# Attention with buffers of its own for the weights before normalising, and a different order around the first scores and the products with values

## The chip, the cores and the metric

The kernel runs on one core of a Trainium2 chip. The metric is the device time of one execution in microseconds (us). The core's engines work side by side, each through its own instructions in order: TensorE (PE) multiplies matrices, VectorE (DVE) and ScalarE (ACT) work element by element, SyncE (SP) issues the transfers, GpSimd (POOL) does little here.

## The reference, cut to what matters

A trunk of two layers over 512 tokens of width 1024, in float32. Layer 0 mixes tokens by native sparse attention, layer 1 by a gated linear recurrence; each mixer stands between two half-step feed-forward networks, and a layer norm follows each of these six parts. The change is in the attention of layer 0:

```python
h = x @ w_in
q, k_c, v_c, k_s, v_s, k_w, v_w, gate = jnp.split(h, ...)
...
o_c = jnp.einsum('bgqtn,bgnd->bgqtd', p_c.astype(dt), vc)
...
l_s = jnp.einsum('bgqtd,bgtsd->bgqts', qb, k_g).astype(F32) * scale + b_s
p_s = _masked_softmax(l_s, (d_s >= 0)[:, :, None])
o_s = jnp.einsum('bgqts,bgtsd->bgqtd', p_s.astype(dt), v_g)
...
return (gb[..., 0:1] * o_c + gb[..., 1:2] * o_s + gb[..., 2:3] * o_w).astype(dt)
...
return o @ w_out
```

There are 16 heads in 4 groups; a group shares its keys and values. Each query has three attentions (over compressed blocks, over selected blocks, over a window), summed with gates. With 512 tokens all blocks are selected and the window reaches over everything, so that the second and third are two causal softmaxes with different keys and values (t = 0 and 1 in the code).

## The kernel before, in words

**Stage.** `nsa_body` first projects keys, values and gates for all groups. Then comes the part that the change touches. Its work is cut into 64 units, in the order: group (4), pair of heads in the group (2), tile of 128 queries `i` (4), head of the pair (2). A pair has 8 units; pair k ends as units 8k to 8k+7 are done.

**Steps.** The loop over n runs in steps; in step n it does, in this order, parts of several units:

- `att_e` for unit n−2: two exponentials on ACT (line 904) turn the scores into unnormalised weights `pe` and sum them up for the denominator (`den`);
- the copies of the product of an earlier step from PSUM to `o` and `o1` on ACT (line 939), queued in `self.last`;
- `att_b` for unit n−3: PE transposes `pe` in blocks of 128x128 (line 917), four to a PSUM bank; ACT copies the first bank to `pt` (line 920), DVE the second (line 922);
- what the tables place at this step (`side`, below);
- `att_a` for unit n: PE computes scores from queries `qs` and keys `kh`, `kl` (lines 882 and 883, 128 queries by up to 512 keys for each t) into banks `sc`; DVE takes the minimum of the far scores (889), adds the bias `near` and takes the minimum (891), whose result `nm` is the exponentials' offset (scores are negated);
- `att_c` for units n−5 and n−4, in odd n−4: PE multiplies the transposed weights with the values into `po` (line 935).

PE executes in the order in which the program is written. The order on the other engines is set by the framework's scheduler, and a transfer waits until its buffer is free.

**PSUM** has 4 banks for scores (`psc`), 3 for all else (`ps`) and 1 for `po`.

**Weights.** `weight` (lines 125 to 135) loads 512 KB into a buffer of `self.raw`, which has three; ACT writes the rounded half `whi` (line 124) and DVE the rest `wlo` (line 125), both into `self.wr`. A product is three matmuls (141 to 143). `self.raw` also holds `rev`, the bias table of a group before it is turned round into `near` (lines 538 to 543), and `pe`.

**Tables.** `PRE` lists what is projected before the first unit: two key weights and the first half (two heads) of group 0's queries. `PLAN` places, for each group, the loads and projections in steps: for groups 1 to 3 the list `Q` relative to step 0, 16 and 32 (load at 0, query projections at 3 and 8, scores against compressed keys at 10 and 11), for group 2 also the keys of groups 2 and 3 (`K`). `FIN` places the end of pair k, relative to step 8k: `factors` (reciprocals of `den` times the gates, DVE), `turned` (PE transposes them, ACT and DVE write them as `rt`, lines 770 to 772), `weigh(0)` and `weigh(1)` (PE spreads `rt` over the head's rows, line 776; DVE multiplies `o` or `o1` by it, 778, and adds both, 780), `compressed` (the first attention's product, 784 and 785) and `o_split`. What lies past the last step is done inside the output projection that follows (`out_proj`).

## Time and profile before

| what | value |
|---|---|
| time, median of 3 runs | 2057.42 us (2056.58 to 2058.37) |
| the profiled execution's own time | 2057.78 us |
| its span, first to last instruction | 2056.0 us |
| mean granted TensorE clock | 0.995 of full speed |
| PE busy | 2005.1 us (98%) |
| DVE busy | 1384.1 us (67%) |
| ACT busy | 1007.4 us (49%) |
| moved by transfers | 193.92 MB, mean 94 GB/s |

The profile is of one execution. The 1.8 us between its time and its span lie before the first and after the last instruction. PE's busy time counts pipelined matmuls as busy from their start to a modelled end. The part that the change touches runs from about 415 to 655 us of the span. In a timeline row the number in square brackets is the time for which the engine stood idle before the instruction, and the arrow names what released it; in the views of waits such times are summed.

### The profile page before, as it was taken

How to read it: one execution, taken by the hardware profiler on the slowest of the kernel's cores; microseconds unless marked ns; L12 is line 12 of the kernel's file. 1: busy time of each engine (PE TensorE's matmuls, PEld its weight loads, DVE VectorE, ACT ScalarE, POOL GpSimd, SP SyncE). 2: the span in 40 equal slices, each digit the busy share in tenths (PEclk: the TensorE clock that was granted, in tenths of full speed). 3: DMA queues.
4: the chain of work that ended last, by engine and by line, in shares of the span. 5: the costliest groups of instructions: out<-in, count | busy, mean ns of one | idle time of the engine just before them, and what ended most of it. 6: DMA issues, size and time to landing. Idle time of an engine off the chain costs nothing.

```text
span 2056.0 us, 36186 instructions
## 1 busy us (share of the span) xinstructions
PE 2005.1 (98%) x15225; PEld 1803.7 (88%) x15225; DVE 1384.1 (67%) x1996; ACT 1007.4 (49%) x1670; POOL 142.0 (7%) x165
## 2 busy tenths in 40 slices
PE   9999999999999999999999999999999999999998
PEld 9998998877777899899899989988887779998996
DVE  8845866366777797477599558663735868955864
ACT  5542553246677355245345435534736844543551
POOL 0000002000000200000020000030412112000002
PEclk9999999999999999999999999999999999999999
DMA  5342342311103235133334423422220043342331
GB/s 185 124 144 62 104 134 70 106 40 42 42 1 114 93 109 174 47 103 93 113 97 130 144 62 103 139 88 90 87 84 2 4 144 103 121 147 62 103 124 41
DMA packets 138768, 193.92 MB, mean 94 GB/s; under 512 B 8572, under 2 KB 117564, under 8 KB 138605
## 3 DMA queue, kind: packets, MB, share of 16 engines
q1 hardware_dynamic: 138604, 191.61, 30.1%
q8 instruction: 119, 1.95, 0.4%
q14 instruction: 45, 0.36, 0.1%
HBM read 189.40 MB, written 2.19 MB: 93 GB/s over the span
## 4 chain that ended last, share of the span: by engine, by line
PE 80%; DVE 11%; ACT 3%; issue 3%; DMA 2%; POOL 1%; SPq 0%; POOLq 0%; DVEq 0%; ACTq 0%
PE ps L141 24%; PE ps L142 23%; PE ps L143 23%; DVE wlo L125 2%; PE ps L364 2%; PE ps L917 2%; PE po L935 1%; DMA fr<-in_ffn_w_up_dram 1%; DVE raw L395 1%; PE sc L882 1%; DVE xl L125 1%; PE ps L183 1%; PE sc L883 1%; POOL ry L220 1%; DVE x L230 1%
## 5 line engine op out<-in xcount | busy, mean ns | idle before, releaser
L125 DVE TENSOR_TENSOR wlo<-raw,whi 128x1024 fp32r<-128x1024 f32 (+1 forms) x253 | 310.9, 1233 | 247.0 <-ACT whi L124 246.6
L124 ACT ACTIVATE whi<-raw 128x1024 fp32r<-128x1024 f32 (+1 forms) x253 | 266.0, 1056 | 324.3 <-PE ps L143 144.8
L141 PE MATMUL ps<-xh,whi 128*128 128x256 f32 (+1 forms) x992 | 296.1, 299 | 1.3 <-ACT xh L124 0.5
L142 PE MATMUL ps<-xl,whi 128*128 128x256 f32 (+1 forms) x992 | 294.6, 297 | 0.7 <-DVE xl L125 0.7
L143 PE MATMUL ps<-xh,wlo 128*128 128x256 f32 (+1 forms) x992 | 294.1, 296 | 0.0
L143 PE MATMUL ps<-whi,xlo 128*128 128x512 f32 x704 | 274.4, 390 | 1.5 <-DVE xlo L125 1.5
L141 PE MATMUL ps<-whi,xhi 128*128 128x512 f32 x704 | 274.4, 390 | 0.0
L142 PE MATMUL ps<-wlo,xhi 128*128 128x512 f32 x704 | 274.0, 389 | 0.0
L141 PEld LDWEIGHTS ps<-xh,whi 128*128 128x128 f32 x992 | 187.7, 189 | 9.7 <-ACT xh L124 1.0
L142 PEld LDWEIGHTS ps<-xl,whi 128*128 128x128 f32 x992 | 187.6, 189 | 7.9 <-DVE xl L125 1.1
L143 PEld LDWEIGHTS ps<-xh,wlo 128*128 128x128 f32 x992 | 187.5, 189 | 6.7
L124 ACT ACTIVATE whi<-fr 128x1024 fp32r<-128x1024 f32 x120 | 126.1, 1061 | 115.4 <-PE ps L142 80.7
L141 PE MATMUL ps<-xh,xhi 128*128 128x256 f32 x640 | 177.6, 278 | 2.7 <-DVE c L450 2.7
L142 PE MATMUL ps<-xl,xhi 128*128 128x256 f32 x640 | 177.2, 277 | 0.0
L143 PE MATMUL ps<-xh,xlo 128*128 128x256 f32 x640 | 177.2, 277 | 0.0
L125 DVE TENSOR_TENSOR wlo<-fr,whi 128x1024 fp32r<-128x1024 f32 x120 | 145.6, 1221 | 44.9 <-ACT whi L124 44.7
L143 PEld LDWEIGHTS ps<-whi,xlo 128*128 128x128 f32 x704 | 132.1, 188 | 30.6 <-DVE xlo L125 3.2
L395 DVE TENSOR_TENSOR raw<-fr 128x1024 f32<-128x1024 f32 x120 | 145.7, 1222 | 17.8 <-DMA fr<-in_ffn_w_up_dram 16.3
L141 PEld LDWEIGHTS ps<-whi,xhi 128*128 128x128 f32 x704 | 132.2, 188 | 26.9
L142 PEld LDWEIGHTS ps<-wlo,xhi 128*128 128x128 f32 x704 | 132.2, 188 | 26.9
L125 DVE TENSOR_TENSOR xlo<-h,xhi 128x1024 fp32r<-128x1024 f32 x44 | 53.9, 1226 | 110.8 <-ACT xhi L124 110.8
L141 PEld LDWEIGHTS ps<-xh,xhi 128*128 128x128 f32 x640 | 120.4, 188 | 3.5 <-DVE c L450 3.5
(279 smaller groups left out, 4635.3 us busy)
## 6 DMA issues: line engine op xcount, KB each, us to landing
raw<-in_ffn_w_down_dram SPq DMA_DIRECT2D x88, 512.0 KB, 3.6
fr<-in_ffn_w_gate_dram SPq DMA_DIRECT2D x80, 512.0 KB, 4.0
fr<-in_ffn_w_up_dram SPq DMA_DIRECT2D x80, 512.0 KB, 5.1
raw<-in_hgrn_w_in_dram SPq DMA_DIRECT2D x32, 512.0 KB, 4.1
raw<-in_nsa_w_in_dram SPq DMA_DIRECT2D x18, 512.0 KB, 3.8
raw<-in_ffn_w_gate_dram SPq DMA_DIRECT2D x8, 512.0 KB, 4.6
raw<-in_ffn_w_up_dram SPq DMA_DIRECT2D x8, 512.0 KB, 4.9
raw<-in_nsa_w_out_dram SPq DMA_DIRECT2D x8, 512.0 KB, 4.5
```

The source lines that it names most:

```text
L124: a = self.nc.scalar.activation(hi, src, AF.Copy)
L125: b = self.nc.vector.tensor_tensor(lo, src, hi.bitcast(F32), op=ALU.subtract)
L141: mm(out, l[0], r[0], start=start, stop=False)
L142: mm(out, l[0], r[1], start=False, stop=False)
L143: mm(out, l[1], r[0], start=False, stop=stop)
L183: self.nc.tensor.transpose(p[:, j, :], self.x[c][:, k * P : (k + 1) * P], self.ident)
L220: self.nc.gpsimd.tensor_tensor(y, y, self.mhalf[:, :n], op=ALU.pow)
L230: nc.vector.scalar_tensor_tensor(x[:, s], x[:, s], float(scale), banks[h], op0=ALU.mult, op1=ALU.add)
L364: nc.tensor.matmul(out, l, xx, start=k == low == 0 and xx is x[0], stop=k == 7 and low == 1)
L395: tt(out, x, y, op=op)
L882: nc.tensor.matmul(sc, l, kh[g][:, ts[0] : ts[0] + x, :n], start=True, stop=False)
L917: nc.tensor.transpose(p[:, j * P : j * P + P], pf[:, (b0 + j) * P : (b0 + j + 1) * P], self.ident)
```

## The change

1. `pe` moves from `self.raw` to two buffers of its own in the attention's pool. The space comes from `pt` (4 buffers to 3), `near` (2 buffers of 4 heads to 3 of 2 heads) and `o1` (2 to 1).
2. `near` is written as two tiles of two heads each by two DVE copies; for groups 1 to 3 its load moves from step 0 of the group's list to step 9.
3. The second half of group 0's queries is projected before the first unit instead of at step 2.
4. In a step, the products with values (`att_c`) come ahead of the scores (`att_a`).
5. At the end of a pair `weigh(1)` comes first, at step 12, then `weigh(0)` at 13, which now also adds `o1`; `compressed` moves from 14 to 15.

```diff
--- before.py
+++ after.py
@@ -52,12 +52,12 @@
 LB = 3
 LC = 4
 
-PRE = [("keys", 0), ("keys", 1), ("queries", 0)]
-Q = [(0, "load", "q"), (3, "queries", 0), (8, "queries", 1), (10, "cmp_a", 0), (11, "cmp_a", 1), (24, "cmp_b")]
+PRE = [("keys", 0), ("keys", 1), ("queries", 0), ("queries", 1)]
+Q = [(0, "load", "q"), (3, "queries", 0), (8, "queries", 1), (9, "load", "near"), (10, "cmp_a", 0), (11, "cmp_a", 1), (24, "cmp_b")]
 K = [(5, "load", 0), (7, "load", 1), (10, "keys", 0), (11, "keys", 1)]
-PLAN = [(0, 0, [(2, "queries", 1), (4, "cmp_a", 0), (4, "cmp_a", 1), (10, "cmp_b")]), (1, 0, Q), (2, 16, Q + K), (3, 32, Q)]
-
-FIN = [(10, "factors", ()), (11, "turned", ()), (13, "weigh", (0,)), (14, "compressed", ()), (15, "weigh", (1,)), (17, "o_split", ())]
+PLAN = [(0, 0, [(4, "cmp_a", 0), (4, "cmp_a", 1), (10, "cmp_b")]), (1, 0, Q), (2, 16, Q + K), (3, 32, Q)]
+
+FIN = [(10, "factors", ()), (11, "turned", ()), (12, "weigh", (1,)), (13, "weigh", (0,)), (15, "compressed", ()), (17, "o_split", ())]
 
 
 class Trunk:
@@ -538,8 +538,9 @@
         rev = self.raw.tile([P, 4, 256], F32, name="rev", tag="raw")
         nd = self.near_d
         nc.sync.dma_start(rev, bass.AP(tensor=nd.tensor, offset=nd.offset + 4 * g * 384, ap=[[1, P], [384, 4], [1, 256]]))
-        near = pool.tile([P, 4, 256], F32, name="near", tag="near", bufs=2)
-        nc.vector.tensor_copy(near, rev[:, :, ::-1])
+        near = [pool.tile([P, 2, 256], F32, name="near", tag="near", bufs=3) for _ in range(2)]
+        for i, t in enumerate(near):
+            nc.vector.tensor_copy(t, rev[:, 2 * i : 2 * i + 2, ::-1])
         return near
 
     def nsa_cb(self, pool):
@@ -687,7 +688,7 @@
             nc.gpsimd.memset(pc, 0.0)
             cb = self.nsa_cb(pool)
             prep = [self.group_prep(pool, w, g, groups[g], pc, cb) for g in range(4)]
-            for t in ("q", 0, 1):
+            for t in ("near", "q", 0, 1):
                 prep[0]["load"](t)
             work = self.ps
             for f, *x in PRE:
@@ -725,7 +726,7 @@
                 exps = []
                 if LE <= n < len(units) + LE:
                     g, hh, i = units[n - LE]
-                    pes[n - LE], exps = self.att_e(opool, groups[g], hh, i)
+                    pes[n - LE], exps = self.att_e(pool, groups[g], hh, i)
                 behind, self.last = self.last, []
                 with self.after(exps[-1:]):
                     for f in behind:
@@ -734,12 +735,12 @@
                         pts[n - LB] = self.att_b(pool, units[n - LB][2], pes.pop(n - LB))
                 for f in side.pop(n, ()):
                     f()
+                if n >= LC and (n - LC) % 2:
+                    g, hh, i = units[n - LC]
+                    self.att_c(opool, groups[g], g, hh // 2, i, [pts.pop(n - LC - 1), pts.pop(n - LC)])
                 if n < len(units):
                     g, hh, i = units[n]
                     self.att_a(pool, g, groups[g], hh, i)
-                if n >= LC and (n - LC) % 2:
-                    g, hh, i = units[n - LC]
-                    self.att_c(opool, groups[g], g, hh // 2, i, [pts.pop(n - LC - 1), pts.pop(n - LC)])
             for f in self.last:
                 f()
             assert not side
@@ -776,8 +777,8 @@
             nc.tensor.matmul(p, spread[:, t].rearrange("p x d -> p (x d)"), rt, start=True, stop=True)
             own = (out, st["o1"][pr])[t]
             tt(own, own, p, op=ALU.mult)
-            if t:
-                tt(out, out, own, op=ALU.add)
+            if t == 0:
+                tt(out, out, st["o1"][pr], op=ALU.add)
 
         def compressed():
             p = self.psum()
@@ -796,8 +797,9 @@
         v, vc, gate, kc, o = self.kv
 
         def load(t):
-            if t == "q":
+            if t == "near":
                 st["near"] = self.nsa_near(pool, g)
+            elif t == "q":
                 st["us"] = self.units(w, 256 * g, 256)
                 st["q"], st["den"], st["o1"], st["sc"] = [], [], [], {}
             else:
@@ -873,7 +875,7 @@
         n = (i + 1) * P
         l = st["q"][hh][:, i * P : i * P + P]
         m = min(n, 256)
-        bias = st["near"][:, hh, 256 - m :]
+        bias = st["near"][hh // 2][:, hh % 2, 256 - m :]
         nm = self.small.tile([P, 2], F32, name="nm", bufs=6)
         out = []
         for ts in ((0, 1),) if i < 2 else ((0,), (1,)):
@@ -898,7 +900,7 @@
             st["den"].append(self.small.tile([P, NT, 2, 2], F32, name="den", bufs=3))
         den = st["den"][hh // 2]
         out, nm = st["sc"].pop((hh, i))
-        pe = self.raw.tile([P, 2, (i + 1) * P], F32, name="pe", tag="raw")
+        pe = pool.tile([P, 2, (i + 1) * P], F32, name="pe", tag="pe", bufs=2)
         exps = []
         for t in range(2):
             ins = self.nc.scalar.activation(pe[:, t, :], out[t], AF.Exp, scale=-1.0, bias=nm[:, t : t + 1], accum_out=den[:, i, hh % 2, t : t + 1])
@@ -908,7 +910,7 @@
     def att_b(self, pool, i, pe):
         nc = self.nc
         nb = 2 * (i + 1)
-        pt = pool.tile([P, nb, P], F32, name="pt", tag="pt", bufs=4)
+        pt = pool.tile([P, nb, P], F32, name="pt", tag="pt", bufs=3)
         pf = pe.rearrange("p t n -> p (t n)")
         for b0 in range(0, nb, 4):
             m = min(4, nb - b0)
@@ -927,7 +929,7 @@
         nc = self.nc
         v, vc, gate, kc, o = self.kv
         if i == 0:
-            st["o1"].append(pool.tile([P, T], F32, name="o1", tag="o1", bufs=2))
+            st["o1"].append(pool.tile([P, T], F32, name="o1", tag="o1"))
         po = self.po[:, i % 2]
         for t in range(2):
             for j in range(i + 1):
```

What the steps become on the engines' instruction lists:

**ACT, the end of group 0's units and the start of group 1's.** `whi<-raw` is the split of a weight, `pe` the exponentials (128x512 of the last units of group 0, 128x128 of the first of group 1), `pt` copies of transposed weights, `o` copies of the product. Before:

```order
L920 ACTIVATE pt<-ps 128x512
L124 ACTIVATE whi<-raw 128x1024
L904 ACTIVATE pe,den<-sc,nm 128x512
L124 ACTIVATE whi<-raw 128x1024
L904 ACTIVATE pe,den<-sc,nm 128x512
L920 ACTIVATE pt<-ps 128x512
L904 ACTIVATE pe,den<-sc,nm 128x128 x2
L939 ACTIVATE o<-po 128x128
L939 ACTIVATE o_4859<-po 128x128
```

Now:

```order
L941 ACTIVATE o<-po 128x128
L941 ACTIVATE o_4854<-po 128x128
L922 ACTIVATE pt<-ps 128x512
L906 ACTIVATE pe,den<-sc,nm 128x512 x2
L922 ACTIVATE pt<-ps 128x512
L906 ACTIVATE pe,den<-sc,nm 128x128 x2
L941 ACTIVATE o<-po 128x128
L941 ACTIVATE o_4854<-po 128x128
L922 ACTIVATE pt<-ps 128x512
```

The two splits of group 2's query weights have left this place; the exponentials stand together.

**SP, the loads of the stage.** `raw` are weights, `rev` the bias table of a group, `cb` that of the compressed keys. Before:

```order
L540 DMA rev<-near_d 128x4x256
L550 DMA cb<-cmp_d 16x16x56 x8
L133 DMA raw<-in_nsa_w_in_dram 128x4x256 x2
L540 DMA rev<-near_d 128x4x256
L133 DMA raw<-in_nsa_w_in_dram 128x4x256 x2
L133 DMA raw<-in_nsa_w_in_dram 128x8x128 x2
L540 DMA rev<-near_d 128x4x256
L133 DMA raw<-in_nsa_w_in_dram 128x4x256 x2
L133 DMA raw<-in_nsa_w_out_dram 128x1024 x6
```

Now:

```order
L133 DMA raw<-in_nsa_w_in_dram 128x4x256
L551 DMA cb<-cmp_d 16x16x56 x8
L133 DMA raw<-in_nsa_w_in_dram 128x4x256
L540 DMA rev<-near_d 128x4x256
L133 DMA raw<-in_nsa_w_in_dram 128x4x256 x2
L133 DMA raw<-in_nsa_w_in_dram 128x8x128 x2
L540 DMA rev<-near_d 128x4x256
L133 DMA raw<-in_nsa_w_in_dram 128x4x256 x2
L540 DMA rev<-near_d 128x4x256
L133 DMA raw<-in_nsa_w_out_dram 128x1024 x7
```

The bias tables of groups 1 to 3 now follow the query weights of the groups, and one more weight of the output projection stands ahead of what follows the stage.

**PE, steps 12 to 14, the end of the first pair.** `po<-pt,v` are products with values, `sc` scores, `ps<-ident,pe` transposes, `ps<-rt,spread` the product of `weigh`, `ps<-pct,vc` that of `compressed`. Before:

```order
L917 MATMUL ps<-ident,pe 128x128 x4
L776 MATMUL ps<-rt,spread 128x512
L882 MATMUL sc<-kh,qs 128x384
L883 MATMUL sc<-kl,qs 128x384
L882 MATMUL sc<-kh,qs 128x384
L883 MATMUL sc<-kl,qs 128x384
L935 MATMUL po<-pt,v_3612 64x128 x4
L917 MATMUL ps<-ident,pe 128x128 x4
L784 MATMUL ps<-pct,vc 128x512
```

Now:

```order
L919 MATMUL ps<-ident,pe 128x128 x2
L777 MATMUL ps<-rt,spread 128x512
L884 MATMUL sc<-kh,qs 128x384
L885 MATMUL sc<-kl,qs 128x384
L884 MATMUL sc<-kh,qs 128x384
L885 MATMUL sc<-kl,qs 128x384
L919 MATMUL ps<-ident,pe 128x128 x4
L777 MATMUL ps<-rt,spread 128x512
L937 MATMUL po<-pt,v_3612 64x128 x4
L884 MATMUL sc<-kh,qs 128x384
```

The first `spread` product now stands behind the two transposes of step 12, the second behind the four of step 13, and the products with values ahead of the scores.

## Rows read from the trace of the kernel before

**Rows 1.** The page, busy time by engine, and its group of weight splits on DVE.

```profile
PE 2005.1 (98%) x15225; PEld 1803.7 (88%) x15225; DVE 1384.1 (67%) x1996; ACT 1007.4 (49%) x1670; POOL 142.0 (7%) x165
...
L125 DVE TENSOR_TENSOR wlo<-raw,whi 128x1024 fp32r<-128x1024 f32 (+1 forms) x253 | 310.9, 1233 | 247.0 <-ACT whi L124 246.6
```

**Rows 2.** Stretches: length, busy us of PE, PEld, DVE, ACT, POOL; clock, DMA share, GB/s.

```profile
454.00:462.00 8.00, 5.64 (x43) 3.65 (x39) 8.00 (x37) 6.02 (x19) 0.00 (x0) 1.00 0.00 0
...
490.00:502.00 12.00, 7.79 (x38) 6.13 (x35) 5.73 (x17) 7.45 (x23) 0.00 (x0) 0.72 0.22 76
...
556.00:568.00 12.00, 7.79 (x50) 6.29 (x49) 6.57 (x20) 7.45 (x23) 0.00 (x0) 0.86 0.29 88
...
sum 240.00, PE 223.84 PEld 177.01 DVE 177.80 ACT 155.38 POOL 0.00; mean PE 22.38 PEld 17.70 DVE 17.78 ACT 15.54 POOL 0.00
```

**Rows 3.** What PE waited for, 415 to 660: us in total, times, longest.

```profile
PE ps L917 <- ACT pe L904: 8.4, 4, 2.8
...
PE sc L882 <- ACT pe L904: 3.3, 5, 1.1
...
PE sc L882 <- DVE qs L826: 2.7, 2, 1.5
...
PE ps L141 <- ACT o L939: 0.6, 1, 0.6
```

**Rows 4.** Timeline of PE: start, length, line, tiles; idle time before and releaser.

```profile
493.53 0.66 PE L917 MATMUL ps<-ident,pe 128*128 128x128 f32 x4 [2.77 <-ACT pe L904]
...
495.62 1.12 PE L917 MATMUL ps<-ident,pe 128*128 128x128 f32 x4 [1.44 <-ACT pe L904]
...
560.42 0.66 PE L917 MATMUL ps<-ident,pe 128*128 128x128 f32 x4 [2.80 <-ACT pe L904]
```

**Rows 5.** Timeline of all engines at the first stall (SPq: SP's DMA queue).

```profile
488.01 1.50 SPq L133 DMA_DIRECT2D raw<-in_nsa_w_in_dram  x2
...
491.75 1.06 ACT L124 ACTIVATE whi<-raw 128x1024 fp32r<-128x1024 f32 x1 [3.41 <-DMA raw<-in_nsa_w_in_dram]
```

**Rows 6.** What SP's queue waited for, 360 to 700.

```profile
SPq L133 <- PE ps L917: 116.1, 9, 88.5
```

**Rows 7.** Stretches of 2 us, columns as in rows 2.

```profile
436.00:438.00 2.00, 2.00 (x7) 1.61 (x6) 0.97 (x5) 2.00 (x6) 0.00 (x0) 0.59 0.01 4
...
494.00:496.00 2.00, 0.56 (x4) 0.38 (x3) 1.40 (x4) 2.00 (x5) 0.00 (x0) 0.59 0.00 0
...
496.00:498.00 2.00, 2.00 (x9) 1.70 (x8) 1.47 (x6) 2.00 (x11) 0.00 (x0) 0.50 0.00 0
...
500.00:502.00 2.00, 2.00 (x8) 1.60 (x7) 0.00 (x0) 0.00 (x0) 0.00 (x0) 0.70 0.00 0
...
562.00:564.00 2.00, 1.51 (x6) 1.37 (x7) 1.65 (x3) 2.00 (x10) 0.00 (x0) 0.66 0.00 0
```

**Rows 8.** Timeline of PE, first and last matmul of an undisturbed query projection.

```profile
583.98 0.50 PE L141 MATMUL ps<-xh,whi 128*128 128x512 f32 x1
...
589.32 0.40 PE L143 MATMUL ps<-xh,wlo 128*128 128x512 f32 x1
```

**Rows 9.** Timeline of PE, scores waiting for a bank in odd steps.

```profile
459.29 0.50 PE L882 MATMUL sc<-kh,qs 128*128 128x512 f32 x1 [0.59 <-ACT pe L904]
...
480.32 0.44 PE L882 MATMUL sc<-kh,qs 128*128 128x384 f32 x1 [0.44 <-ACT pe L904]
```

**Rows 10.** Timeline of PE, DVE and ACT around the end of the first pair.

```profile
477.49 0.68 DVE L772 TENSOR_TENSOR rt<-ps,rt 4x512 fp32r<-4x512 f32 x1
...
477.52 0.42 PE L882 MATMUL sc<-kh,qs 128*128 128x384 f32 x1
...
482.61 0.43 ACT L939 ACTIVATE o<-po 128x128 f32<-128x128 f32 x2
...
487.01 0.68 DVE L780 TENSOR_TENSOR o<-o,o 128x512 f32<-128x512 f32 x1
```

**Rows 11.** Timeline of ACT at the end of the stage.

```profile
649.45 2.05 ACT L124 ACTIVATE whi<-raw 128x1024 fp32r<-128x1024 f32 x2
```

## Prediction

> **What bounds the kernel now.** I began with the page: over the whole span TensorE (PE) is busy for 98%, VectorE (DVE) for 67% [rows 1]. A change that removes no matmul can only gain where PE stands still or runs slowly, so I next cut the attention stage (about 415 to 655 us of the span) into stretches. Two of twelve microseconds stand out, 490 to 502 and 556 to 568: in each PE works 7.79 us, at a mean granted clock of 0.72 and 0.86; and between 454 and 462 it is DVE that is full, 8.00 of 8.00; over the whole stage PE is idle for 240 − 223.84 = 16.2 us [rows 2]. Then I asked what PE waits for. The largest entry is the transposes of the unnormalised weights (`ps`, line 917) waiting for ACT's exponentials (`pe`): 8.4 us in four waits. After it come scores waiting for exponentials (3.3 us in five: their PSUM banks are still being read), scores waiting for `qs` (2.7 in two) and the output projection waiting for the last copy of `o` (0.6) [rows 3].
>
> The timeline of PE places the 8.4 us: 2.77 and 1.44 near 493 us, 2.80 and the remaining 1.4 near 560 us [rows 4]. ACT shows why. Between two exponentials stands the split of a weight, `whi<-raw`, and ACT sat idle for 3.41 us until that weight's load landed; the loads were issued only at 488.01 [rows 5]. They could not go earlier: `pe` and weight loads rotate through the same three buffers of `raw`, so a load waits until the transposes have read an old `pe`. SP waited 116.1 us for those transposes in all [rows 6]. ACT executes in its order, so the exponentials behind `whi` wait for a load that has nothing to do with them.
>
> The stall costs twice. PE waits, and then it runs at the lower granted clock: 0.59 in the window that starts at 494, 0.50 from 496 to 500, 0.70 in the window after [rows 7]; 0.50 is the 1.2 GHz level, 1.00 the 2.4 GHz level. The same fall follows the pause before the first scores: 0.59 from 436 to 438 and about the same in the two us after [rows 7].
>
> **The change, part by part.** The profiled execution took 2057.78 us, 0.36 above the median of the runs. I sum against 2057.78.
>
> *Own buffers for `pe`.* With `pe` out of `raw`, SP can issue the loads of groups 2 and 3 much earlier, and the order on ACT shows the effect: no `whi` is left among the exponentials of units 15 and 31, the last of groups 0 and 1. Both stalls should go. First: idle 2.77 + 1.44 = 4.21; at the low clock, lost share times PE's busy time, 0.41 × 0.56 + 0.5 × 2 + 0.5 × 2 + 0.3 × 2 = 2.83 [rows 7], the window from 498 like the one from 496. Second: idle 2.80 + 1.4 = 4.2; clock 0.34 × 1.51 [rows 7] + 0.5 × 2 for the window after it = 1.5. Together 7.04 + 5.7 = **−12.7**. A lower bound for what is lost is the idle time alone, 8.4. No matmul, exponential or load is added or dropped here.
>
> *Where the loads go instead.* The splits of group 2's queries and first key weight now stand in the first steps, and those of the output weights in the attention stage. Each costs 1.06 us on ACT and 1.23 on DVE [rows 1, 5]. Most stand next to a projection of 24 matmuls, which keeps PE busy by itself for 5.74 us (583.98 to 589.72) [rows 8]. The tight one is the key weight at step 5: its load takes the buffer that the split of a query weight frees. That split ends some 2.2 us into the projection (1.0 for work ahead of it, an estimate, and 1.23); the load takes 3.74 from issue to the start of `whi` (488.01 to 491.75), and 1.06 + 1.23 follow: 8.2 us, against 5.74 of projection and about 1.5 of scores and transposes behind it. I take **+1.0**, bounds 0 and 2.5 (8.2 − 5.74).
>
> *Second query projection ahead of the first scores.* Before, PE pauses 1.46 + 1.22 us for `qs` (the 2.7 of [rows 3]) and then loses 0.41 × 2 by the clock in one window and about as much in the next, 1.6: 4.3 in all. Afterwards the first scores find the first `qs` long ready, but the pause may return at the first transposes: ACT must finish the copies of the second projection and a `whi` before it comes to the first exponentials. All 24 matmuls run in either version. I take **0**, the pause coming back in the size that it has now: the 2.7 is the nearest row. Bounds: −3.3 (one us of pause is left) and +2.2 (a `whi` and a DVE copy more).
>
> *Products with values ahead of the next scores.* Of the five waits of scores for a bank, those of odd steps, 0.59 and 0.44 among them [rows 9], now have products in front of them. They sum to 1.5 at most. The waits near 455 sit where DVE is full, so they partly return; and moving scores back by up to 2 us shortens the lead of DVE and ACT. I take **−0.8**, bounds −1.5 and 0.
>
> *Pair end.* The first `spread` product moves from step 13 or later to step 12, straight behind two transposes. It needs DVE's half of `rt`, which ended at 477.49 + 0.68 = 478.17, while PE was past these transposes at 477.52 [rows 10]: 0.65 us. I compared all pairs: the same in one other (the fifth), no wait in the other five. 2 × 0.65 = 1.3, part of which takes the place of the later 0.44 wait; I take **+0.8**, bounds 0 and 1.3. `o1` goes from two buffers to one: ACT's first copy of the next pair waits until DVE has read the old `o1`. The new order puts that read and the sum of both right behind step 13; I take **+0.3**, bounds 0 and the rival below.
>
> *Halved `near`.* Two copies of 128x512 for one of 128x1024, four times, all on DVE and beside projections: 0. Its cover would be gone only where DVE is full already.
>
> *End of the stage.* Two `whi` (2.05 us) stand before ACT's last copies of `o` [rows 11], for which the output projection waits 0.6 [rows 3]. These splits are done earlier now: **−0.5**, bounds −0.64 and 0.
>
> Sum: −12.7 + 1.0 + 0 − 0.8 + 0.8 + 0.3 − 0.5 = **−11.9**, that is 2045.9 in the terms of the profiled execution, 2045.5 in those of the median.
>
> The trace shows PE idle for 4.2 us in each stall, although it is the engine with the most work [rows 1, 4].
> The Trainium skill (Perfetto Trace Analysis, Identifying the Most-Contended Engine) says to optimize the engine with the highest occupancy first, and warns that for TensorE matmul busy time is a poor measure. By that rule alone the change, which takes no work off PE, would give next to nothing, 2057. The rows of PE's idle time say otherwise, and the sum is made from them.
>
> **The rivals.** *The wait moves (0.15).* The loads come earlier, but ACT or DVE stands before a load that has not landed elsewhere: at step 5, where the bound is 2.5, or at step 24, where the load of an output weight waits for DVE's second copy of `near`. One such wait as long as one old stall gives back 5.7 to 7.0: a gain of 5 to 6, about 2052. For it: the 8.2 against 5.74 above. Against: the projections beside both places.
>
> *DVE takes over (0.08).* If the exponentials wait for DVE's minima, as in 454 to 462, whatever the loads do, then PE's idle time appears under scores or transposes again. For it: DVE is full in that stretch, and gets 3 splits there early. Against: in 490 to 502 it works 5.73 of 12.00 us [rows 2]. The gain would fall to 0 to 4: about 2055. That the loads don't move at all is no case any more: the order shows them moved.
>
> *Slower (0.05): one buffer for `o1`.* ACT's copy into `o1` has the next exponentials behind it. If DVE reads the old `o1` as late as before, at 487.01 + 0.68 = 487.69, while the first copies of the next pair stood at 482.61 [rows 10], ACT waits about 4.9 us (from after the first of the two copies). How much it can wait unnoticed is shown by the stall: held for 3.41 + 1.06 us it cost PE 2.77 [rows 4, 5], so 1.7 is slack. At seven pair ends 7 × 3.2 = 22: −11.9 + 22 gives **2068**. It decides from a wait of 1.7 us. Against it: the read has been moved to steps 12 and 13, close to 482.
> The Trainium skill (Trainium Kernel Development and Optimization, Best Practices) advises double buffering for performance, which speaks against this one part; whether a trace bears it out no run here shows yet.
>
> **How the numbers follow.** My forecast, both stalls gone and nothing as large in their place, gets 0.72; the wait that moves 0.15, DVE 0.08, slower 0.05. A measurement can tell about 0.2%, 4.1 us, from no change. The first two cases are faster by more: 0.87; the third is the same: 0.08; the last slower: 0.05. The forecast's own bounds are −12.7 − 3.3 − 1.5 − 0.64 = −18.1 and −12.7 + 2.5 + 2.2 + 1.3 + 0.3 = −6.4: 2039.7 to 2051.4 (the 0.36 aside). That holds the forecast and about half of the first rival; I give 2039.5 to 2051.5, and 2045.5 as the likeliest.
>
> **What would show it.** Right: the 8.4 us entry is gone from PE's waits, the projections of groups 2 and 3 start at a granted clock of 1.00, PE is idle under 8 us between 415 and 655 (16 before), and SP's waits on transposes are gone. The step-5 price shows as PE waiting for a `ps` bank after the second group's first projection; the pair end as `spread` waiting for DVE's `rt`; `o1` as an ACT wait for DVE ahead of a copy. The prediction fails if an ACT row `whi` with idle time for a load stands between exponentials again, or if PE's idle time only changes its name.

## The result and the profile after

| | before | changed |
|---|---|---|
| median, 7 runs each | 2057.42 us (2051.37 to 2058.37) | 2045.63 us (2040.92 to 2048.53) |
| ratio, with its 95% interval | | 0.9946 (0.9931 to 0.9961) |
| profiled execution: time | 2057.78 | 2040.92 |
| profiled execution: span | 2056.0 | 2039.1 |
| PE busy | 2005.1 | 1998.2 |

The change saves 11.8 us by the medians; the interval is 8.0 to 14.2. The forecast was 2045.5. The two profiled executions differ by more, 16.9, since that of before lies near the upper end of its kernel's runs and that of the changed kernel is its lowest; where the difference lies is worked out below.

What PE waited for in the attention stage, in the changed kernel (total us, times, longest):

```profile
PE ps L919 <- ACT pe L906: 2.6, 1, 2.6
PE sc L884 <- ACT pe L906: 2.6, 3, 1.2
PE ps L777 <- DVE o L779: 1.0, 1, 1.0
PE ps L141 <- ACT pt L922: 0.9, 1, 0.9
```

Against [rows 3], the 8.4 us in four waits have become 2.6 in one, and that one is new: it is the pause before the very first transposes. The waits for `qs` and for the last copy of `o` are gone, and scores wait for exponentials nearly as long as before (2.6 us in place of 3.3). New are a wait of `spread` for DVE and one of a projection for ACT, 1.9 together.

The timeline of ACT at the place of the first stall, once the last units of group 0 are done:

```profile
483.53 0.69 ACT L906 ACTIVATE pe<-sc,nm 128x512 f32<-128x512 f32 x1
...
484.21 0.68 ACT L906 ACTIVATE pe<-sc,nm 128x512 f32<-128x512 f32 x1
...
484.87 0.59 ACT L922 ACTIVATE pt<-ps 128x512 f32<-128x512 f32 x1
...
485.46 0.37 ACT L906 ACTIVATE pe<-sc,nm 128x128 f32<-128x128 f32 x1
```

Against [rows 5] the two `whi` with their idle time for a load are gone; the exponentials follow one another without a pause. The clock stays up too. These are the stretches around the two old stalls (columns as in rows 2):

```profile
482.00:490.00 8.00, 7.74 (x66) 6.59 (x65) 5.88 (x25) 7.30 (x28) 0.00 (x0) 1.00 0.00 0
548.00:556.00 8.00, 8.00 (x52) 6.66 (x49) 2.83 (x15) 4.24 (x17) 0.00 (x0) 1.00 0.01 2
```

The granted clock is 1.00 in both, where the stretches of before show 0.72 and 0.86 [rows 2].

SP's queue in the changed kernel, each row a run of transfers from its first issue to its last:

```profile
417.03 24.38 SPq L133 DMA_DIRECT2D raw<-in_nsa_w_in_dram  x4
444.69 0.37 SPq L540 DMA_DIRECT2D rev<-near_d  x1
458.74 3.77 SPq L133 DMA_DIRECT2D raw<-in_nsa_w_in_dram  x2
```

The four loads for group 2 (queries and keys) leave between 417.03 and 441.4, the two for group 3 by 462.5; before, the query weights left at 488.01 [rows 5] and near 555.

**Where the time went, unit by unit.** To lay two executions on top of each other, I took the start of each unit's transposes on PE and measured it from one point ahead of the stage, the products of the compression's hidden layer (393.97 before, 389.39 in the changed kernel, so 4.58 us are taken off). The differences, changed minus before:

```
after unit's transposes start   before    changed   difference less 4.58
 1                              449.45    444.70    -0.2
 4                              457.88    453.61    +0.3
14                              488.01    482.83    -0.6
17                              507.74    496.13    -7.0
23                              526.59    515.04    -7.0
30                              554.88    546.23    -4.1
33                              573.61    559.05   -10.0
63                              647.38    632.89    -9.9
in a feed-forward part behind   823.23    807.80   -10.8
```

Two drops of about 6 us stand where the stalls were, one rise of 2.9 between units 23 and 30, and small steps elsewhere. So the stage and the start of the output projection give 10.8 us. Of the other 6 us between the two profiles, 4.58 had arisen before the stage began, and the rest lies behind it; nothing of the change lies in either (the last section).

### The profile page after: what moved, and what is told of

Its sections match the earlier page's. It is cut to its first block, busy times and chain, and to the rows that moved or that the text cites. A ratio compares the mean times of both kernels' runs of the same rounds, so it can differ in the third digit from the quotient of the medians.

```text
span 2039.1 us, 36202 instructions
## 1 busy us (share of the span) xinstructions
PE 1998.2 (98%) x15225; PEld 1797.9 (88%) x15225; DVE 1380.7 (68%) x2000; ACT 1007.2 (49%) x1670; POOL 141.9 (7%) x165
## 4 chain that ended last, share of the span: by engine, by line
PE 79%; DVE 11%; ACT 4%; issue 3%; POOL 2%; DMA 1%; POOLq 0%; SPq 0%; DVEq 0%; ACTq 0%
PE ps L141 24%; PE ps L143 23%; PE ps L142 23%; DVE wlo L125 2%; PE ps L364 2%; PE po L937 2%; PE ps L919 1%; PE sc L884 1%; DVE raw L395 1%; DVE xl L125 1%; PE ps L183 1%; POOL ry L220 1%; PE sc L885 1%; DVE xlo L125 1%; ACT whi L124 1%
```

## The experiments

All are variants of the changed kernel, so a difference is against that kernel, and units are compared in the way of the table above. The times of whole runs scatter by some microseconds. By units, the control at the end agrees with the first profile of the changed kernel to 0.2 us; each variant has one profile.

One thing differs between these profiles that the edits do not explain. I call the steps up to unit 14 the fill. PE pauses in it, and behind a pause the granted clock falls to 0.50 (the 1.2 GHz level) in some profiles and not in others. These are two us of the changed kernel, behind its first pause of 2.65 us, and two of the run below that holds back the splits of the output weights, behind its first pause of 2.64 us (columns as in rows 2):

```profile
438.00:440.00 2.00, 2.00 (x6) 1.63 (x5) 0.68 (x2) 1.75 (x5) 0.00 (x0) 0.50 0.17 41
```

```profile
439.00:441.00 2.00, 2.00 (x10) 1.68 (x9) 0.73 (x1) 1.23 (x3) 0.00 (x0) 1.00 0.42 111
```

| run | PE's first pause (us) | clock falls to 0.50 behind it | falls near unit 5 |
|---|---|---|---|
| changed kernel, and the control | 2.65, 2.65 | yes, yes | no, no |
| `pe` in `raw` | 1.83 | no | no |
| bias table at step 0 | 3.61 | yes | yes |
| both undone | 3.63 | yes | no |
| second projection at step 2 | 1.46 and 1.22 | yes | no |
| scores first | 2.65 | yes | yes |
| old table of pair ends | 2.65 | yes | no |
| output weights' splits held | 2.64 | no | yes |
| the same, compressed scores at step 8 | 2.64 | no | no |
| more splits held | 1.83 | yes | no |
| the same, compressed scores at step 6 | 1.83 | no | no |

A fall costs 1.4 to 1.6 us in each place. After pauses of the same length it comes in one profile and not in another, and what decides it no run here shows. So 1.6 us in the fill is not a price of an edit, and the readings below say where it is in them.

### Where the stalls went: two parts of the change, undone singly and together

`pe` back in `raw`:

```diff
-        pe = pool.tile([P, 2, (i + 1) * P], F32, name="pe", tag="pe", bufs=2)
+        pe = self.raw.tile([P, 2, (i + 1) * P], F32, name="pe", tag="raw")
```

> The changed kernel with one part undone: pe takes its tile from the three buffers of raw again. Theory (the sharing of raw makes both stalls): two ACT rows whi with 3 us or more of idle time for a load come back among the exponentials of units 15 and 31, PE loses about 6.5 and 6 us there, and the time rises by 11 to 14 us, to about 2057 or 2058. Rival (another part, such as the later load of near, removed the stalls): no such rows, time within 3 us of the changed kernel.

Measured: 2048.29 us (2046.94 to 2048.91), ratio to before 0.9958 (0.9941 to 0.9974). The stage ends only 1.2 us later, or 2.8 if the fall of the clock that this profile lacks is added. My theory fell here, and the rival stood. The timeline of this kernel, SP's queue and ACT:

```profile
477.82 25.85 SPq L133 DMA_DIRECT2D raw<-in_nsa_w_in_dram  x4
...
483.10 0.69 ACT L906 ACTIVATE pe<-sc,nm 128x512 f32<-128x512 f32 x1 [0.80 <-DVE nm L893]
...
483.77 1.05 ACT L124 ACTIVATE whi<-raw 128x1024 fp32r<-128x1024 f32 x1
...
484.72 0.68 ACT L906 ACTIVATE pe<-sc,nm 128x512 f32<-128x512 f32 x1
...
485.38 1.05 ACT L124 ACTIVATE whi<-raw 128x1024 fp32r<-128x1024 f32 x1
```

Both splits are back among the exponentials, but ACT does not wait for a load: SP issued it at 477.82, 7.4 us earlier than at 488.01 [rows 5] when both are measured from the common point. What is left are the two splits themselves, and units 15 to 17 lose 2.3 us by them, units 31 to 33 as much. The fill gained 2.9 (units 3 to 7): 1.6 because the clock did not fall, and 1.3 that fits group 2's splits no longer standing in it. Units 23 to 27 win 2.7, which the last experiments explain; 1.9 is lost at unit 22, behind a projection that waits 1.67 us for ACT's copy of `pt`.

The other part, the bias table at step 0 of its list again, ahead of the query weights, while `pe` keeps its own buffers:

```diff
-Q = [(0, "load", "q"), ..., (9, "load", "near"), ...]
+Q = [(0, "load", "near"), (0, "load", "q"), ...]
```

> The changed kernel with the bias table of a group loaded at step 0 of its list, ahead of the query weights, as before the change; pe keeps its own buffers. After the first experiment there are two theories of why PE's stalls went. A (own buffers are enough: the loads leave early whatever the table does): units 15 to 17 and 31 to 33 stay within 1 us of the changed kernel, time within 2 us of it. B (the table's load, which stood ahead of the weights in SP's queue and held a buffer of raw, made the wait): ACT waits 2 us or more for a load at one of these places or in the first steps, and the time rises by 4 to 12 us.

Measured: 2046.61 us (2044.70 to 2050.94), ratio 0.9966 (0.9955 to 0.9977). No stall at units 15 to 17 or 31 to 33 (0.4 us each); as A says, own buffers are enough for them. But the fill loses 3.5 us by unit 8, 1.6 of it by the second fall of the clock, and the stage ends 4.2 us later. That is in the range of B, though the ACT wait of 2 us for a load, by which B would come, is not there. PE's longest pauses are these:

```profile
441.38 0.68 PE L919 MATMUL ps<-ident,pe 128*128 128x128 f32 x2 [3.61 <-ACT pe L906]
...
458.03 0.50 PE L884 MATMUL sc<-kh,qs 128*128 128x512 f32 x1 [2.07 <-ACT pe L906]
```

The first was 2.65 in the changed kernel, the second 1.16.

Both undone:

> Both parts undone: pe in raw and the table at step 0 of its group's list; all else as in the changed kernel. Theory (either part alone removes ACT's wait for the load, only own buffers also take the two splits out of the row of exponentials): ACT waits about 3.4 us for a load at units 15 and 31, PE loses 6 to 7 us at each as before the change, and the time is 10 to 13 us above the changed kernel. Rival (the stalls went by the order of scores and products, or by the pair ends): under 5 us above it.

Measured: 2059.32 us (2056.86 to 2064.11), ratio 1.0024 (1.0013 to 1.0036), so a little slower than before the change. ACT's timeline:

```profile
488.17 1.06 ACT L124 ACTIVATE whi<-raw 128x1024 fp32r<-128x1024 f32 x1 [2.71 <-DMA raw<-in_nsa_w_in_dram]
...
490.49 1.06 ACT L124 ACTIVATE whi<-raw 128x1024 fp32r<-128x1024 f32 x1 [1.26 <-DMA raw<-in_nsa_w_in_dram]
...
558.64 1.06 ACT L124 ACTIVATE whi<-raw 128x1024 fp32r<-128x1024 f32 x1 [3.32 <-DMA raw<-in_nsa_w_in_dram]
```

and SP's queue:

```profile
480.99 0.37 SPq L540 DMA_DIRECT2D rev<-near_d  x1
484.66 1.96 SPq L133 DMA_DIRECT2D raw<-in_nsa_w_in_dram  x2
```

The stalls are whole again: 6.9 us from unit 14 to 17 and 6.5 from 30 to 33; the stage ends 13.7 us later. The rows show the chain: the table takes the next free buffer of `raw` (480.99), and the weights leave when the buffers after that are free (484.66). In the run with `pe` in `raw` and the table at step 9 the first weight left 7.1 us earlier from the common point, 3.4 of which is the faster fill. Whether the table also delays the weights by its place in SP's queue alone, no run separates. The two parts are substitutes for the most part:

| end of the stage, against the changed kernel | table at step 0 | table at step 9 |
|---|---|---|
| `pe` in `raw` | +13.7 | +1.2 |
| `pe` in its own buffers | +4.2 | 0 |

The +1.2 has one fall of the clock less in the fill than the changed kernel, the +4.2 one more. Without them they would be about +2.8 and +2.6, so either part alone takes some 11 of the 13.7 us, and which of them is worth more is not shown.

With both undone the stage ends 3.8 us later than in the kernel before (13.7 against 9.9), and 2.3 of that is lost between units 17 and 23. So the other parts cost something there as long as `pe` is in `raw`; which of them (the order, the pair ends, three buffers for `pt`, the halved `near`) no run shows. The three buffers of `pt` and the halved `near` were never undone by themselves.

### The other parts

The second query projection at step 2 again:

```diff
-PRE = [("keys", 0), ("keys", 1), ("queries", 0), ("queries", 1)]
+PRE = [("keys", 0), ("keys", 1), ("queries", 0)]
...
-PLAN = [(0, 0, [(4, "cmp_a", 0), ...
+PLAN = [(0, 0, [(2, "queries", 1), (4, "cmp_a", 0), ...
```

> The changed kernel with the second half of group 0's queries projected at step 2 again. Theory (the pause of PE before the first transposes replaced one of the same size before the first scores): PE's pauses before unit 1's transposes sum to about 2.7 us as before, in two pieces that wait for qs, and the landmarks from unit 3 on lie within 1 us of the changed kernel's; time 2045 to 2047. Rival (this part earned time): 2 us or more lost by unit 4.

Measured: 2045.77 us (2045.13 to 2048.90), ratio 0.9949 (0.9932 to 0.9967). PE's pauses are 1.46 and 1.22 for `qs`, in place of the one of 2.65; from unit 2 to the end of the stage the units lie 0.2 to 0.4 us ahead of the changed kernel. This part is worth nothing, as forecast; at the end of the stage it costs 0.4.

The scores ahead of the products again (the two blocks of the loop change places):

```diff
+                if n < len(units):
+                    g, hh, i = units[n]
+                    self.att_a(pool, g, groups[g], hh, i)
                 if n >= LC and (n - LC) % 2:
...
-                if n < len(units):
-                    g, hh, i = units[n]
-                    self.att_a(pool, g, groups[g], hh, i)
```

> The changed kernel with the scores of a step ahead of its products with values again. Theory: waits of scores for a bank in odd steps come back, 0.5 to 1.5 us in all between units 4 and 12, and little else; time 0 to 2 us above the changed kernel. Rival (products ahead leave DVE and ACT a shorter lead, and cost at the pair ends): the 1.0 us wait for DVE's o near the fourth pair end goes, and the time falls by 1 us or more.

Measured: 2049.59 us (2045.12 to 2051.16), ratio 0.9962 (0.9948 to 0.9976). Unit 5 loses 1.6 us, by the second fall of the clock; unit 14 stands at +3.2, the end of the stage at +2.0. The rival's gain at the fourth pair end is there (the 1.03 us wait is gone, units 26 to 27 win back 0.9), but is outweighed. So the order of products and scores is worth 2.0 us if that fall is its doing, and 0.4 if not; the forecast was 0.8. One profile does not tell which.

The old table of pair ends with one buffer for `o1`:

```diff
-FIN = [..., (12, "weigh", (1,)), (13, "weigh", (0,)), (15, "compressed", ()), ...]
+FIN = [..., (13, "weigh", (0,)), (14, "compressed", ()), (15, "weigh", (1,)), ...]
...
-            if t == 0:
-                tt(out, out, st["o1"][pr], op=ALU.add)
+            if t:
+                tt(out, out, own, op=ALU.add)
```

> The changed kernel with the old table of pair ends (weigh(0) at 13, compressed at 14, weigh(1) at 15 with the sum), while o1 keeps its one buffer. The slower rival of the prediction priced this: ACT's copy into o1 waits for DVE's late sum, about 4.9 us, less 1.7 us of slack, at up to seven pair ends: 10 to 22 us more than the changed kernel, with ACT rows o1 that wait for DVE. If the slack is larger than worked out: under 3 us more.

Measured: 2069.87 us (2066.58 to 2073.03), ratio to before 1.0069 (1.0047 to 1.0090); the stage ends 23.8 us later. What PE waited for in this kernel's stage:

```profile
PE po L937 <- ACT o L941: 17.6, 7, 2.9
PE ps L919 <- ACT pe L906: 2.6, 1, 2.6
```

and ACT at the first pair end:

```profile
484.53 0.28 ACT L941 ACTIVATE o<-po 128x128 f32<-128x128 f32 x1 [0.47 <-DVE o L781]
...
486.88 0.45 ACT L941 ACTIVATE o<-po 128x128 f32<-128x128 f32 x2 [2.07 <-PE po L937]
```

Seven waits, one at each of seven pair ends, 2.5 us each. The other 6.2 us come mostly by the clock, which stays at 1.00 there in the changed kernel and falls behind five of the seven waits. Behind the first:

```profile
486.00:488.00 2.00, 2.00 (x11) 1.48 (x9) 0.00 (x0) 0.45 (x2) 0.00 (x0) 0.50 0.00 0
```

This is the slower rival, whose 22 us and 2068 this run bears out in size. One detail was otherwise: PE waits less for exponentials behind the copy than for `po` itself, the one bank that the held copy has to empty before the next products.
The Trainium skill (Trainium Kernel Development and Optimization, Best Practices) advises double buffering for performance, to overlap DMA with compute.
`o1` is not loaded by DMA, but the question is the same. In this case one buffer with the late reader costs 23.8 us, and with the read at steps 12 and 13 no copy of `o1` waits for DVE. The kernel before, with two buffers and the late reader, has no such wait of PE either.

### The 2.9 us lost between units 23 and 30

PE in the changed kernel at this place:

```profile
525.61 0.50 PE L141 MATMUL ps<-xh,whi 128*128 128x512 f32 x1 [0.91 <-ACT pt L922]
...
537.48 0.50 PE L777 MATMUL ps<-rt,spread 36*128 36x512 f32 x1 [1.03 <-DVE o L779]
```

and the splits of output weights, on ACT and on DVE, ahead of them:

```profile
512.00 1.06 ACT L124 ACTIVATE whi<-raw 128x1024 fp32r<-128x1024 f32 x1 [1.66 <-PE ps L142]
...
523.01 1.06 ACT L124 ACTIVATE whi<-raw 128x1024 fp32r<-128x1024 f32 x1 [2.67 <-PE ps L142]
...
532.29 1.23 DVE L125 TENSOR_TENSOR wlo<-raw,whi 128x1024 fp32r<-128x1024 f32 x1
```

They start as soon as a projection has freed their buffers, and stand ahead of copies (`qs`, `kh`, `pt`) and of DVE's minima that PE needs soon. So I held them back by order alone:

```diff
+                if n - LE == 38:
+                    self.hold = exps[-1:]
...
-        us = [self.weight(...) for k in range(NK)]
+        with self.after(self.hold):
+            us = [self.weight(...) for k in range(NK)]
```

> The changed kernel with the splits of the output weights on ACT ordered behind the exponentials of unit 38, instead of steps 24 to 27 (loads unchanged). Theory (these three splits, 1.06 us each on ACT and 1.23 on DVE, are the 2.9 us that the change loses between units 23 and 31): PE's waits of 0.91 and 1.03 us near 525 and 537 go, units 27 to 31 come 2 to 3 us earlier, and up to 1 us is lost again near unit 40 or at the start of the output projection; time 1 to 3 us under the changed kernel. Rival (the pair end or the second group's keys make that loss): those units move by under 0.7 us.

Measured: 2041.57 us (2040.75 to 2048.01), ratio 0.9938 (0.9918 to 0.9958). Between units 23 and 28 the kernel gains 2.45 us of the 2.9, and the waits of 0.91 and 1.03 are gone (0.20 is left): shown. It gives most of that back. In the fill it gains 1.6 because the clock does not fall behind the first pause, and loses 2.6 by a fall near unit 5 and a longer wait for `qs` (1.29 in place of 0.32). It loses 0.9 and 0.8 more at units 40 and 44, behind four splits that now stand together (568 to 579 us). The stage ends 0.6 us earlier; the rest of the better median does not come from the stage.

The same, with the second half of group 0's compressed scores at step 8 instead of 4:

```diff
-PLAN = [(0, 0, [(4, "cmp_a", 0), (4, "cmp_a", 1), ...
+PLAN = [(0, 0, [(4, "cmp_a", 0), (8, "cmp_a", 1), ...
```

> As the run before, and the second half of group 0's compressed scores moves from step 4 to step 8, ahead of a projection. Theory (DVE, full between units 4 and 6, holds up scores there: 1.16 and 0.67 us): both waits shrink to under 0.5 us in all, units 6 to 15 come 1 to 1.8 us earlier than in the run before. Rival (the waits are set by ACT's exponentials, which come late by their own work): no change there.

Measured: 2039.77 us (2039.57 to 2043.20), ratio 0.9935 (0.9917 to 0.9953). Units 4 and 5 come 2.5 and 4.0 us earlier than in the run before, but the work that was moved holds up step 8, and from unit 8 on 1.8 us remain. The waits of scores did not vanish, they are 0.71, 0.57 and 0.32 now. The gain is of the expected size, but 1.4 of it is the fall of the clock near unit 5 that the run before has and this one lacks, so the theory is not shown by it.

Holding the splits of group 2 as well, and those of the output weights in two places:

```diff
+            with self.after(self.ex.get({0: 33, 1: 33, 2: 38, 3: 38}.get(k), ())):
+                us.append(self.weight(...))
...
+                    held = f.func is prep[2]["load"] and f.args[0] != "near"
+                    with self.after(self.ex[5] if held else ()):
+                        f()
```

> The changed kernel with splits held back by order alone: those of group 2's query and key weights behind the exponentials of unit 5, the first two output weights' behind those of unit 33, the next two behind unit 38. Theory (a split on ACT costs PE where it stands ahead of exponentials or copies that PE needs soon, and nothing beside a projection): the 2.65 us pause before the first transposes falls to about 1.6, units 1 to 8 come 1.5 to 3 us earlier, units 27 to 31 2 to 3 us more, and the 0.9 us waits that the run with all splits at unit 38 had at units 40 and 44 go; the stage ends 3.5 to 5.5 us earlier than in the changed kernel. Rival (the splits moved to step 8 hold up DVE's minima there): units 8 to 12 lose the first gain again.

Measured: 2042.97 us (2041.34 to 2044.72), ratio 0.9935 (0.9920 to 0.9949). The first pause falls to 1.83, the units from 4 to 9 come 1.3 us earlier, but by unit 12 all of that is lost, as the rival said: ACT waits 1.27 and 0.78 us for DVE ahead of exponentials, and PE 0.88 for one of these. The 2.4 at units 23 to 28 are there, the wait at unit 44 is gone, that at 40 is not. The stage ends 1.75 us earlier, not 3.5 to 5.5: a miss.

The last, with the second half of the compressed scores at step 6:

```diff
-PLAN = [(0, 0, [(4, "cmp_a", 0), (4, "cmp_a", 1), ...
+PLAN = [(0, 0, [(4, "cmp_a", 0), (6, "cmp_a", 1), ...
```

> As the run before, with the second half of group 0's compressed scores at step 6 instead of 4. Theory: DVE, full between units 4 and 6, is relieved, and another 0.5 to 1.5 us come by unit 8. Rival: it is full at step 6 as well, and nothing comes.

Measured: 2040.93 us (2039.99 to 2042.27), ratio to before 0.9925 (0.9910 to 0.9940). By unit 8 it is 1.6 us ahead of the run before, but it is so at unit 1 already, ahead of the work that was moved: there the clock did not fall. The moved work itself gives 2.0 us by unit 4, and by unit 8 they are lost again, so the theory is not shown here either. The stage ends 4.2 us earlier than in the changed kernel, 2.6 without the clock. Its runs (2039.99 to 2042.27) all lie below those of the control in the same series (2044.31 to 2051.19).

The control:

> The changed kernel once more, as it is. If the differences between executions come from elsewhere than the attention stage, its units lie within 0.1 us of the first profile once the start of the stage is laid on top, while the whole time differs by some microseconds.

Measured: 2048.19 us (2044.31 to 2051.19), ratio 0.9954 (0.9940 to 0.9968). All units lie within 0.2 us of the first profile (0.1 was expected), while the two profiled executions differ by 7.3 us as a whole.

## Why the prediction was right, and where it was not

The time came out right, 2045.63 against 2045.5. That it came out to 0.1 us is luck: a cost of 2.9 us that the sum has at nothing was made up in part by a cost at the pair end that did not come (1.1) and by smaller differences, and the medians differ by 1 us more than the stage does. By the unit table:

| term of the sum | forecast | measured | read between |
|---|---|---|---|
| the two stalls | −12.7 | −6.4 and −5.9 | units 14 and 17, 30 and 33 |
| second query projection ahead | 0 | −0.2 | the common point and unit 1 |
| splits in the fill | +1.0 | +0.5 | units 1 and 4 |
| products ahead of scores | −0.8 | −0.9 | units 4 and 14 |
| pair end (`rt`, `o1`) | +1.1 | 0 | no such wait |
| splits at steps 24 to 27 | 0 | +2.9 | units 23 and 30 |
| end of the stage | −0.5 | −0.9 | unit 33 and the part behind |
| sum | −11.9 | −10.9 | |

The small terms of the fill are nets of several parts. Undone one by one these are: group 2's splits 1.3 us (the run that holds them, units 4 to 9), the table's move, which the sum does not have, some 2 by unit 8 without the clock, the order of products and scores 0.4 or 2.0.

PE's idle time in the stage fell less than the prediction named as a sign of being right, under 8 us; it is 225.00 − 216.09 = 8.9, against 16.2 before [rows 2]:

```profile
415.00:640.00 225.00, 216.09 (x1579) 171.06 (x1578) 173.65 (x561) 158.44 (x458) 0.00 (x0) 0.99 0.15 46
```

The other signs came: of the 8.4 us only the new 2.6 is left, the clock is at 1.00 where the stalls were, and no wait of SP on transposes of `pe` is left. The 2057 that the prediction names for a change that takes no work off PE did not come, since what the change takes away is idle time and low clock of that engine.

**The stalls** were sized well: idle time and the loss by the clock together made 12.7, against 12.3. The rows that were read for it, PE's idle time and the window's granted clock, were enough to price these two.

**Their cause was told incompletely.** The part of the prediction on own buffers says that loads "could not go earlier" because `pe` and the loads share `raw`. True, but the table of biases was the other half: it went into SP's queue ahead of the weights, and took the buffer that they could have had. The rows of before have it, in the view of rows 6 and in SP's timeline:

```profile
SPq L540 <- PE ps L917: 100.5, 2, 63.8
...
484.62 0.37 SPq L540 DMA_DIRECT2D rev<-near_d  x1
```

The table waits 63.8 us for a buffer, leaves at 484.62, and the weights at 488.01. Of the 116.1 us that the prediction quotes for the weights, 88.5 is one later wait of the output weights. The table's move from step 0 to step 9 was read in the order of SP's list and never priced. The four runs show that either part alone takes ACT's long wait away, and that each alone is worth about 11 us of stage without the clock's falls in the fill (9.5 for the buffers and 12.5 for the table as measured).

**The pause at the start** came back as forecast: 2.65 us before the first transposes for the 2.7 before the first scores [rows 3], with the same loss of clock behind it in this kernel's two profiles (0.50 from 438 to 440). The run with the second projection at step 2 bears that out. The tight load at step 5 did make ACT wait, and the projection covered it almost wholly:

```profile
436.63 0.68 PE L919 MATMUL ps<-ident,pe 128*128 128x128 f32 x2 [2.65 <-ACT pe L906]
...
442.34 1.06 ACT L124 ACTIVATE whi<-raw 128x1024 fp32r<-128x1024 f32 x1 [2.58 <-DMA raw<-in_nsa_w_in_dram]
...
447.90 0.66 PE L919 MATMUL ps<-ident,pe 128*128 128x128 f32 x4 [0.32 <-DVE qs L828]
```

**The pair end** was costed for a wait for `rt` that does not occur: no matmul with `spread` waits for `rt` after, and the one `spread` wait there is (1.03) went when the splits were held. The kernel with the old ends puts the price on the other side: had the sum not been moved with the buffer, the change would have made the kernel slower (ratio 1.0069).

**The step that failed** is the sentence that most of the moved splits stand next to a projection, with the price of nothing for all but the one at step 5. Here a split that waits for the projection's own buffers starts when the projection frees them, and is then ahead of copies that PE wants next: 2.9 us are lost at this place, and holding the splits back gives 2.45 of them again. The first rival named step 24, but for a load that had not landed; the load was there, the work of the split was the cost.

## What to carry to other kernels

When a transfer is late, ask what stands ahead of it in the turn of its buffers, not only whose buffer it waits for: here a small transfer that was moved away was worth about as much as buffers of its own. When loads become early, the work on them (splits, casts, copies) becomes early too; price where it lands on each engine, and hold it by order where it lands between a projection's end and the copies that follow it. A buffer may be given up if its reader is moved with it, and both have to be done together. Before two profiles are compared by parts, read the granted clock of each part: 1.6 us in the fill came and went with it, after pauses of the same length.

## What the runs showed that I had not expected

In the feed-forward parts the same matmuls run at two paces, at the same granted clock. PE is busy throughout in both of these stretches, of the profile of before and of the profile after:

```profile
80.00:130.00 50.00, 50.00 (x426) 50.00 (x426) 34.35 (x37) 27.07 (x37) 0.00 (x0) 1.00 0.54 168
```

```profile
80.00:130.00 50.00, 50.00 (x444) 50.00 (x443) 34.81 (x38) 28.12 (x38) 0.00 (x0) 1.00 0.52 168
```

In 50 us one executes 426 matmuls and the other 444, 4% more, with no wait between them. Nothing of the change lies there. Such stretches, each worth some 2 us, occur in some executions and not in others, in each of the feed-forward parts; this one makes up some 2 of the 4.58 us by which the two profiles differ before the stage. That such stretches also make the scatter of the runs without a profile is likely and not shown. What sets the pace was not found. For a change of a few microseconds it means that parts of two profiles should be laid on a common point ahead of them before they are compared: for the changed kernel that repeats to 0.2 us here, while whole runs differ by 7.
